# One chain of heads across the block borders, other yield distances in S5, and the short convolution of blocks 2 and 3 moved into the delta-rule groups

## The chip, the cores and the metric

The kernel runs on one core of a Trainium2 chip. The metric is the device time of one execution in microseconds (us). The kernel before took 2914.17 us (median of 3 runs, 2912.3 to 2915.87).

A core has several engines that each work through a queue of their own in order: TensorE (PE, matrix products; PEld is its weight load), VectorE (DVE), ScalarE (ACT), GpSimd (POOL) and SyncE (SP, which here issues the DMAs). An instruction waits at the head of its queue until what it needs is there, and all that stands behind it on the same engine waits with it.

## The reference

One layer of a hybrid encoder runs over 2048 prompt tokens and 32 decode tokens of a second request group, model width 1024, float32. All three mixers read the same normalised input through one projection; their outputs go together through `w_out`:

```python
hn = rmsnorm(h, norm_mix);  proj = hn @ w_in
qkv_pre, z, ba, u5, cc = split(proj)
ya = gdn_mixer(qkv_pre, z, ba, ...)   # short causal conv (4 taps) + silu on q, k, v; delta rule, 4 heads x 128
yb = s5_mixer(u5, ...)                # diagonal SSM, 16 groups, gelu, GLU
yc = conformer_conv(cc, ...)          # GLU, depthwise conv of 31 taps, LayerNorm, swish
h = h + concat([ya, yb, yc]) @ w_out
hf = rmsnorm(h, norm_ffn)
h = h + (silu(hf @ ffn_w1) * (hf @ ffn_w3)) @ ffn_w2
h = h + (p @ pe_w) * sigmoid(h @ pe_gate_w)
y = rmsnorm(h, norm_final)
```

The delta rule carries a 128 x 128 state per head along the tokens, and S5 a complex state, so both go through the blocks in order. The 32 decode tokens have states of their own.

## The kernel before

**Blocks and phases.** The 2080 tokens are cut into four blocks of 512 columns; the last also holds the 32 decode tokens and has 544, worked in two pieces of 272. Phase A (`PhaseA.block`) runs for blocks 0 to 3 and makes the projections: u5, the conformer's gate and value, twelve q/k/v tiles (`conv`, L592-620) and four z tiles. Phase F (`PhaseF.block`, L1107-1223) then runs for blocks 0 to 3: `w_out`, the 22 hidden tiles of the FFN, `w2`, the layer embedding and its gate. Every weight product is split into high and low parts and made in three passes (`dense`, L104, its matmuls at L120): a matmul of 128 x 512 is one of 528 in a phase A block and of 2016 in an F block, 272 columns wide twice over in block 3. These are the *dense* matmuls below.

**Heads.** Between the two phases stand the heads, which only need phase A's results and must be done before `w_out` of their block:
- `s5_init` (L207) builds the tables of S5 once; `s5_unit` (L415) runs S5 for two blocks at a time (unit 0: blocks 0 and 1; unit 1: blocks 2 and 3). It makes four rounds of ps_v, a scan on DVE that ends in X, and ps_y; after every second round a gelu that ends in gq; at the end ps_glu.
- `conformer_block` (L791), called conf(b) below: 31 taps on DVE for each of two channel halves (cacc, L812-813), PE transposes (ps_ct, L824), LayerNorm statistics on DVE, a scaling on POOL (L840), PE transposes back (ps_cf, L843), affine and swish on ACT and DVE (cxn), and the store to mixT (L852).
- `gdn_group` (L855): the delta rule for 256 tokens, two groups a block, gdn(b) below; in block 3 a further group for the 32 decode tokens. It normalises, makes kk and the matrix U, transposes v (ps_vt, L928), sends U through DRAM, solves row by row on DVE (ct, cx, L951-952), doubles the inverse on PE (ps_q, ps_z), then per 128 tokens ps_ks, ps_vn, ps_s, ps_o, a normalisation, a transpose (ps_ot, L1078), the gate (zy, L1079) and the store to mixT (L1080).

**How data goes between them.** Phase A writes the convolved and silu'd q/k/v to a DRAM tensor `sild`, the gated z to `zgd`, the conformer's input to `xcd`. All heads write to `mixT[b]` in DRAM. `PhaseF.block(b)` begins with eight loads hb<-mixT (L1124), each split into fah and fal, after which the same buffers are loaded with the residual (L1126); the first dense product of `w_out` needs all eight.

**Who sets the order.** The heads are Python generators. `G.start` puts one into a list of chains; `dense` calls `G.step` with its columns, and every 9216 columns (18 matmuls of 512) each chain in the list is advanced by one (L1251-1269). A chain that has just yielded n sleeps for n advances; so the yields say how far apart its parts are placed among the dense matmuls. A phase A block brings about 29 advances, an F block 112. `G.flush()` advances all chains until they are done. A scheduler then fixes each engine's queue at build time, from priorities (dense work and heads alike run in the lowest class, `later`, in the order they were issued), a model of times, and the memory pools. The heads' pools open and close with the generator (`cc_b`, `gd_b`, `s5_u`, one stack side), so a head that starts later can have to wait for the memory of an earlier one.

Before, the order at top level was this: block 0 of phase A; `s5_init` without yields, in a class ahead of `later`; then one chain conf(0), gdn(0) from block 1 and `s5_unit` 0 from block 2; a flush after block 3. F block b starts the chain conf(b+1), gdn(b+1), to which F block 0 adds S5 unit 1 at its end, and each F block ends with a flush. So nothing of a head was left over a border.

Of the kernel before, what the change touches and what calls it, by code (L numbers as in the profile page):

```python
# [206 lines left out]
def s5_init(G, A, tp, pspool):  # L207
# [84 lines left out]


# [25 lines left out]


# [41 lines left out]


# [51 lines left out]
def s5_unit(G, A, u, wp, pspool):  # L415
# [14 lines left out]
    for jq in range(4):  # L430
# [18 lines left out]
        yield 2  # L449
# [56 lines left out]
        yield 2  # L506
# [31 lines left out]
        yield 2  # L538
# [24 lines left out]
class PhaseA:  # L563


    def __init__(self, G, A, ctx):
# [55 lines left out]
    def block(self, b):  # L622
# [92 lines left out]
        with G.later():  # L715
            for g in gs:
                for _ in g:
                    pass
# [3 lines left out]
        for h in range(NH):  # L722
            self.conv(8 + h, 8 + h, b, hf, hl_, bc, n, last, t0)
        for h in range(NH):
            w = load_weight(G, A.w_in[12 + h], KD, "z", h)
            zz = wp.tile([P, n], F32, tag="gacc", name="zz")
            for c0, cn in chunks_of(n):
                cs = slice(c0, c0 + cn)
                p_ = dense(G, G.psD, "pd", w, hf, hl_, ks, c0, cn)
                V.tensor_tensor(zz[:, cs], p_[:, :cn], bc[:, cs], op=ALU.mult)  # L730
            th = wp.tile([P, n], F32, tag="gth", name="zth", bufs=1)
            nc.scalar.activation(th, zz, AF.Tanh, scale=0.5)
            V.scalar_tensor_tensor(zz, th, 1.0, zz, op0=ALU.add, op1=ALU.mult)
# [121 lines left out]
def gdn_group(G, A, sp, pspool, T, tw, nt, nw, S, b, c_out):  # L855
# [106 lines left out]
    yield 3  # L962
# [264 lines left out]
def trunk_kernel(ctx: ExitStack, tc: tile.TileContext, A):  # L1227
# [57 lines left out]
    G.sild = [dd.tile([P, 12, n], F32, tag=f"sild{b}", name=f"sild{b}") for b, n in enumerate(G.ns)]  # L1285
# [85 lines left out]
    with ExitStack() as cx:  # L1371
        pa = PhaseA(G, A, cx)
        pa.block(0)
        with R("s5i") as tp, G.heads():
            s5_init(G, A, tp, G.psM)

        with R("s5_0") as w5:
            G.start(run(conf_of(0), gdn_of(0)))
            for b in range(1, NB):
                if b == G.UB:  # L1380
                    G.start(s5_unit(G, A, 0, w5, G.psM))
                pa.block(b)
            if NB == G.UB:
                G.start(s5_unit(G, A, 0, w5, G.psM))
# [124 lines left out]
```

## Time and profile before

| | |
|---|---|
| median of 3 runs | 2914.17 us (2912.3 to 2915.87) |
| profiled execution, own time | 2906.6 us |
| its span | 2904.8 us |
| mean granted clock of TensorE | 0.976 |
| PE busy | 2775.6 us, 96% |
| DVE busy | 1769.2 us, 61% |
| ACT busy | 931.4 us, 32% |
| POOL busy | 625.4 us, 22% |
| PE idle, in the first 707 us (phase A) | 66 us |
| PE idle, 1160 to 1385 us (end of F block 0, start of F block 1) | 28 us |

The span is the time from the first to the last recorded instruction of one profiled execution. In a row of the profile, `out<-in` are the program's names without buffer numbers, `128x512` the partitions by elements of the output, and a time in square brackets the idle time of the engine ahead of that row with what ended it. "busy" of PE includes time in which it ran at a lower granted clock; the clock stands beside it in the table of stretches.

### The profile page before, as it was taken

The page shows a single profiled execution, that of the slowest core. Times are in us where ns is not written, and L with a number is a line of the kernel's source. Part 1 is how long each engine was busy: PE and PEld are TensorE (multiplying, and loading weights), DVE is VectorE, ACT ScalarE, POOL GpSimd, SP SyncE. Part 2 cuts the span into 40 slices and gives each one's busy share as a digit, 9 for nine tenths or more (in the row PEclk, how much of TensorE's full clock was granted, in tenths as well). Part 3 has the DMA queues.
Part 4 walks back from the last instruction along what each step waited for, and adds up shares of the span by engine and source line. Part 5 has one row for each costly group of instructions (what it writes and reads, how often), then busy time and mean ns, then how long its engine had stood idle before and what let it go on. Part 6 is the DMA issues. An engine that isn't in the chain of part 4 may idle for free.

```text
span 2904.8 us, 40874 instructions
## 1 busy us (share of the span) xinstructions
PE 2775.6 (96%) x15300; PEld 2373.5 (82%) x15300; DVE 1769.2 (61%) x3812; ACT 931.4 (32%) x1382; POOL 625.4 (22%) x482
## 2 busy tenths in 40 slices
PE   7789999899999999898999999999999999999997
PEld 5668777798878778676888887888888789999997
DVE  8989768896675856676663645954454543333343
ACT  4244433334322222233322323432222343222232
POOL 5733222133543434441010100110000010000000
PEclk9989999999999999899999999999999999999998
DMA  6577776657654546565565656765565574555553
GB/s 217 186 261 245 234 206 222 190 169 242 218 176 161 187 152 225 172 205 204 190 199 160 208 167 222 243 203 179 186 190 167 178 269 158 175 174 175 175 188 104
DMA packets 280566, 565.16 MB, mean 195 GB/s; under 512 B 68993, under 2 KB 128529, under 8 KB 280225
## 3 DMA queue, kind: packets, MB, share of 16 engines
q1 hardware_dynamic: 280368, 562.55, 60.1%
q8 instruction: 121, 1.98, 0.3%
q14 instruction: 77, 0.62, 0.1%
HBM read 457.67 MB, written 104.20 MB: 193 GB/s over the span
## 4 chain that ended last, share of the span: by engine, by line
PE 73%; DVE 14%; DMA 8%; issue 2%; SPq 2%; ACT 1%; POOL 0%; DVEq 0%; ACTq 0%; POOLq 0%
PE ps_d L120 65%; DVE gacc L614 1%; DVE cx L952 1%; DMA sild<-gacc 1%; DMA cu<-ud 1%; DVE ct L951 1%; PE ps_q L982 1%; DMA xk<-in_xT 1%; DMA mixT<-zy 1%; PE ps_z L995 1%; DVE cacc L813 1%; PE ps_kk L904 1%; DMA zy<-zgd 1%; DVE X L498 1%; PE ps_ks L1025 1%
## 5 line engine op out<-in xcount | busy, mean ns | idle before, releaser
L94 ACT ACTIVATE wh_w<-wr_w 128x1024 fp32r<-128x1024 f32 (+1 forms) x272 | 281.3, 1034 | 841.3 <-PE ps_d L120 596.5
L120 PE MATMUL ps_d<-fah,wh_w 128*128 128x512 f32 (+1 forms) x1760 | 382.0, 355 | 7.8 <-DVE hb L1142 3.4
L120 PE MATMUL ps_d<-fal,wh_w 128*128 128x512 f32 (+1 forms) x1760 | 379.2, 354 | 0.0
L120 PE MATMUL ps_d<-fah,wl_w 128*128 128x512 f32 (+1 forms) x1760 | 375.5, 352 | 0.0
L120 PEld LDWEIGHTS ps_d<-fah,wh_w 128*128 128x128 f32 x1760 | 290.7, 189 | 52.4 <-issue 4.9
L120 PEld LDWEIGHTS ps_d<-fal,wh_w 128*128 128x128 f32 x1760 | 291.4, 189 | 42.7
L120 PEld LDWEIGHTS ps_d<-fah,wl_w 128*128 128x128 f32 x1760 | 290.8, 188 | 42.8
L1187 DVE TENSOR_TENSOR hb<-hb,ps_d 128x512 f32<-128x512 f32 (+1 forms) x240 | 140.1, 585 | 181.7 <-PE ps_d L120 180.7
L120 PE MATMUL ps_d<-acth,wh_w 128*128 128x512 f32 (+1 forms) x880 | 208.3, 355 | 8.0 <-DVE hb L1187 4.5
L96 POOL TENSOR_TENSOR wl_w<-wr_w,wh_w 128x1024 fp32r<-128x1024 f32 (+1 forms) x68 | 160.7, 2365 | 237.3 <-ACT wh_w L94 229.5
L120 PE MATMUL ps_d<-acth,wl_w 128*128 128x512 f32 (+1 forms) x880 | 209.4, 354 | 0.0
L120 PE MATMUL ps_d<-actl,wh_w 128*128 128x512 f32 (+1 forms) x880 | 209.1, 355 | 0.0
L813 DVE SCALAR_TENSOR_TENSOR cacc<-xc,cc_w,cacc 128x512 f32<-128x512 f32 (+1 forms) x240 | 178.8, 779 | 0.0
L120 PEld LDWEIGHTS ps_d<-acth,wh_w 128*128 128x128 f32 x880 | 148.8, 189 | 34.3 <-DVE hb L1187 6.9
L120 PEld LDWEIGHTS ps_d<-actl,wh_w 128*128 128x128 f32 x880 | 150.1, 190 | 22.4
L120 PEld LDWEIGHTS ps_d<-acth,wl_w 128*128 128x128 f32 x880 | 149.8, 189 | 22.3
L1170 DVE SCALAR_TENSOR_TENSOR fth<-ps_d,bc 128x512 f32<-128x512 f32 (+1 forms) x110 | 64.8, 589 | 135.4 <-PE ps_d L120 134.8
L1165 DVE TENSOR_TENSOR fa<-ps_d,bc 128x512 f32<-128x512 f32 (+1 forms) x110 | 64.7, 589 | 128.8 <-PE ps_d L120 115.5
L1168 DVE SCALAR_TENSOR_TENSOR fa<-fth,fa 128x512 f32<-128x512 f32 (+1 forms) x110 | 92.3, 839 | 73.4 <-ACT fth L1167 73.2
L614 DVE SCALAR_TENSOR_TENSOR gacc<-raw,cw,gacc 128x512 f32<-128x512 f32 (+1 forms) x144 | 118.9, 828 | 27.4 <-ACT gacc L612 24.8
L1173 DVE TENSOR_TENSOR actl<-fa,acth 128x512 fp32r<-128x512 f32 (+1 forms) x110 | 85.5, 778 | 48.6 <-ACT acth L1172 48.4
L120 PE MATMUL ps_d<-hh,wl_qkv 128*128 128x512 f32 (+1 forms) x480 | 108.2, 362 | 5.9 <-POOL wl_qkv L96 5.9
(468 smaller groups left out, 4817.1 us busy)
## 6 DMA issues: line engine op xcount, KB each, us to landing
wr_w<-in_w SPq DMA_DIRECT2D x256, 512.0 KB, 4.0
wl_w<-lo_w SPq DMA_DIRECT2D x192, 512.0 KB, 3.5
lo_w<-wl_w SPq DMA_DIRECT2D x64, 512.0 KB, 3.0
wr_qkv<-in_w_in SPq DMA_DIRECT2D x48, 512.0 KB, 4.0
wl_qkv<-lo_qkv SPq DMA_DIRECT2D x36, 512.0 KB, 4.3
wr_out<-in_w_out SPq DMA_DIRECT2D x32, 512.0 KB, 4.9
wr_gate<-in_pe_gate SPq DMA_DIRECT2D x32, 512.0 KB, 4.6
sild<-gacc SPq DMA_DIRECT2D x48, 256.0 KB, 4.1
```

What stands on the lines that cost most here:

```text
L94: nc.scalar.activation(wh, wr, AF.Copy)
L96: nc.gpsimd.tensor_tensor(wl, wr, wh.bitcast(F32), op=ALU.subtract)
L120: nc.tensor.matmul(ps[:, :cn], a[:, i, :], x(k)[:, c0:c0 + cn], start=start and p_ == 0 and i == 0, stop=stop and p_ == 2 and i == K - 1)
L498: V.tensor_tensor(X[h][half[i], :, 1:], a[half[h], :, :NC], b_[half[h], :, :NC], op=op)
L614: V.scalar_tensor_tensor(acc, raw[:, t:t + W], cw[:, m, t:t + 1], acc, op0=ALU.mult, op1=ALU.add)
L813: V.scalar_tensor_tensor(acc[:, j], xc[:, j, t:t + W], cn_.w[:, j, t:t + 1], acc[:, j], op0=ALU.mult, op1=ALU.add)
L904: nc.tensor.matmul(kk4[:, h - h0], kq[:, 2 * h, cw], kq[:, 2 * h:2 * h + 2, cw], start=True, stop=True)
L1165: V.tensor_tensor(a, p1[:, :cn], bc[:, cs], op=ALU.mult)
L1168: V.scalar_tensor_tensor(a, th, 1.0, a, op0=ALU.add, op1=ALU.mult)
L1170: V.scalar_tensor_tensor(th, p3[:, :cn], 0.5, bc[:, cs], op0=ALU.mult, op1=ALU.mult)
L1173: V.tensor_tensor(fb[:, cs], a, fa[:, cs].bitcast(F32), op=ALU.subtract)
L1187: V.tensor_tensor(hb[m][:, c0:c0 + cn], hb[m][:, c0:c0 + cn], p_[:, :cn], op=ALU.add)
```

## The change

Six edits (the lines of after.py stand some 9 to 53 further down; L822 there is L813 of before):
1. `s5_init` becomes a generator with ten yields or so. It heads a chain `first_heads`: `s5_init`, gdn(0), conf(0), in that order, started before block 1; the conformer is now last. `first_s5` starts at block 2 and waits until the memory of S5 is open. Their flush stands after block 3 as before.
2. One chain `later_heads` runs over all F blocks: conf(1), gdn(1), conf(2), S5 unit 1, gdn(2), conf(3), gdn(3). Ahead of F block b it is only advanced until gdn(b) is done, so a head may go on over a border.
3. The yields in `s5_unit` go from 2, 2, 2 to 3, 4, and 1 or 5; the yield behind the row solve in `gdn_group` from 3 to 5.
4. For blocks 2 and 3 (`G.raw`), `conv` stores its raw tile and returns. `gdn_group` loads three raw tiles, makes the four taps (ACT and three DVE instructions per tile and head), tanh and the silu product, with four further yields of 2 a group.
5. The rest of the gates' computation (`for _ in g`) comes after the twelve conv tiles, not before them.
6. The conv's weights become a constant of the whole kernel.

By its yields, `first_heads` needs 93 advances where blocks 1 to 3 bring some 90, and `later_heads` needs 342 up to the end of gdn(3) where F blocks 0 to 2 bring 336.

```diff
--- before.py
+++ after.py
@@ s5_unit @@
-        yield 2
+        yield 3
...
-        yield 2
+        yield 4
...
-        yield 2
+        yield 1 if jh == 0 else 5
@@ PhaseA.conv @@
+        if b in G.raw:
+            nc.sync.dma_start(G.sild[b][:, jj], raw)
+            return
@@ gdn_group @@
+    if b in G.raw:
+        c0 = c_out + (3 if c_out >= BLK else 0)
+        raws = [sp.tile([P, 4, nn + 3], F32, tag=tg, name="raw" + tg, bufs=1) for tg in ("AQ", "X", "XT")]
+        for i in range(3):
+            nc.sync.dma_start(raws[i], G.sild[b][:, 4 * i:4 * i + 4, c0:c0 + nn + 3])
+        yield 2
+        for i, dst in enumerate((kq[:, 0:4], kq[:, 4:8], vf)):
+            for x in range(4):
+                m = 8 + x if i == 2 else (2 * i + x // 2) + (4 if x % 2 == 0 else 0)
+                a = dst[:, x]
+                nc.scalar.activation(a, raws[i][:, x, 0:nn], AF.Copy, scale=G.cw[:, m, 0:1])
+                for t in range(1, 4):
+                    V.scalar_tensor_tensor(a, raws[i][:, x, t:t + nn], G.cw[:, m, t:t + 1], a, op0=ALU.mult, op1=ALU.add)
+            th = sp.tile([P, 4, nn], F32, tag="U", name="cth", bufs=1)
+            nc.scalar.activation(th, dst, AF.Tanh)
+            V.scalar_tensor_tensor(dst, th, 1.0, dst, op0=ALU.add, op1=ALU.mult)
+            yield 2
...
-    yield 3
+    yield 5
@@ top level, phase A @@
-        with R("s5i") as tp, G.heads():
-            s5_init(G, A, tp, G.psM)
-        with R("s5_0") as w5:
-            G.start(run(conf_of(0), gdn_of(0)))
...
+        def first_heads():
+            with R("s5i") as tp:
+                yield from s5_init(G, A, tp, G.psM)
+            with R("s5_0") as w5:
+                box["w5"] = w5
+                yield from gdn_of(0)
+                yield from conf_of(0)
+                while "done" not in box:
+                    yield 1
@@ top level, phase F @@
-            G.start(run(conf_of(nb), gdn_of(nb), *(s5_of(u) ...)))
-        pf.block(b)
-        G.flush()
+    def later_heads():
+        for b in range(1, NB):
+            yield from conf_of(b)
+            if b % G.UB == 0:
+                yield from s5_of(b // G.UB)
+            yield from gdn_of(b)
+            ready[0] = b
+    G.start(later_heads())
+    for b in range(NB):
+        G.flush(lambda: ready[0] >= b)
+        pf.block(b)
```

The order of the queues at the border between phase A and phase F, on DVE. Before, behind the last z tile (zz; L730 its eviction, L733 its gate) come the splits of F block 0 (fal, L1105), the end of conf(1) (cxn_7722) and the first eviction of `w_out` (hb, L1142):

```order
L730 TENSOR_TENSOR zz_6987<-ps_d_6988,bc_5114 128x272
L730 TENSOR_TENSOR zz_6987<-ps_d_7014,bc_5114 128x272
L1105 TENSOR_TENSOR fal_7077<-hb_7085,fah_7069 128x512
L1105 TENSOR_TENSOR fal_7079<-hb_7095,fah_7071 128x512
L1105 TENSOR_TENSOR fal_7081<-hb_7105,fah_7073 128x512
L1105 TENSOR_TENSOR fal_7083<-hb_7115,fah_7075 128x512
L1105 TENSOR_TENSOR fal_7084<-hb_7120,fah_7076 128x512
L733 SCALAR_TENSOR_TENSOR zz_6987<-zth_7040,zz_6987 128x544
L851 SCALAR_TENSOR_TENSOR cxn_7722<-cth_7724,cxn_7722 128x512
L1142 TENSOR_TENSOR hb_7085<-hb_7085,ps_d_7134 128x512
```

After, at the same place (L739 and L742 are L730 and L733 of before, L822 the taps; cacc_6213 is conf(0), cacc_6936 conf(1); L836 to L844 are conf(0)'s statistics, L860 its swish):

```order
L739 TENSOR_TENSOR zz_6709<-ps_d_6710,bc_4744 128x272
L822 SCALAR_TENSOR_TENSOR cacc_6213<-xc_6210,cc_w_149,cacc_6213 128x512
L739 TENSOR_TENSOR zz_6709<-ps_d_6742,bc_4744 128x272
L822 SCALAR_TENSOR_TENSOR cacc_6936<-xc_6934,cc_w_149,cacc_6936 128x512 x2
L822 SCALAR_TENSOR_TENSOR cacc_6213<-xc_6210,cc_w_149,cacc_6213 128x512 x2
L822 SCALAR_TENSOR_TENSOR cacc_6936<-xc_6934,cc_w_149,cacc_6936 128x512
L742 SCALAR_TENSOR_TENSOR zz_6709<-zth_6784,zz_6709 128x544
L822 SCALAR_TENSOR_TENSOR cacc_6213<-xc_6210,cc_w_149,cacc_6213 128x512 x46
L836 BN_STATS cst_6749<-ctk_6743 128x6
L837 BN_AGGR cmv_6744<-cst_6749 128x2
```

Behind the last eviction of phase A now stand 51 taps, 48 of them conf(0)'s, and then all of conf(0)'s statistics; before, conf(0) was long done there. The store of conf(0) to mixT[0] and behind it the eight loads hb<-mixT[0] stand on SP after that.

The same at the border between F blocks 2 and 3, on PE. Before, ps_vn of the decode group stood among the `w2` products (acth, actl) of F block 2, 288 dense matmuls ahead of the block's end:

```order
L120 MATMUL ps_d<-acth,wh_w_19996 128x512 x4
L120 MATMUL ps_d<-acth,wl_w_19997 128x512 x4
L120 MATMUL ps_d<-actl,wh_w_19996 128x512 x4
L1038 MATMUL ps_vn<-rk,X 32x128 x4
L120 MATMUL ps_d<-acth,wh_w_20030 128x512 x2
L120 MATMUL ps_d<-acth,wl_w_20031 128x512 x2
```

After (L1065, L1079, L1105 are L1038, L1052, L1078 of before), between the last gate product of F block 2 and the first of `w_out` of block 3:

```order
L120 MATMUL ps_d<-fah,wh_gate 128x512 x8
L120 MATMUL ps_d<-fah,wl_gate 128x512 x8
L120 MATMUL ps_d<-fal,wh_gate 128x512 x8
L1065 MATMUL ps_vn<-rk,X 32x128 x4
L149 MATMUL ps_ss<-ones,ssum_20034 128x1 x4
L1072 MATMUL ps_s<-vn,rk 128x128 x4
L1079 MATMUL ps_o<-Sd_19706,kq 32x128
L1080 MATMUL ps_o<-vn,AQ 32x128
...
L132 MATMUL ps_bc<-ident,rso 128x128 x4
L1105 MATMUL ps_ot<-ident,o 128x32 x4
L120 MATMUL ps_d<-fah,wh_out 128x272 x22
```

The last part of the decode group, ps_vn to ps_ot, moved from among dense products to behind all of them; ps_vt of the same group stands 124 dense matmuls ahead of the border. In S5 unit 1 the dense matmuls between ps_v and the ps_y that needs X are 51, 48, 54, 51 before (at the end of F block 0) and 75, 47, 55, 52 after (at the start of F block 1); between the last ps_y and the second group of ps_glu 112 before and 92 after. Between the last ps_ot of gdn(2) and the border of F blocks 1 and 2 stand 58 dense matmuls after.

More of the change, by code (lines that the diff above doesn't have):

```diff
@@ L318, in s5_init @@
     cmul(nc, [x[:, :, :16] for x in big], Bre, Bim, bre0, bim0, bc(kre), bc(kim))
+    yield 1
     C.Hre = cp.tile([P, 8, 9, 16], F32, tag="Hre", name="Hre")
@@ L327, in s5_init @@
         cmul(nc, tmp, C.Hre[:, :, l], C.nHim[:, :, l], cre0, cim0, bc(Lre[:, l]), bc(Lim[:, l]))
+        if l % 3 == 2:
+            yield 1
     V.tensor_scalar(C.nHim, C.nHim, -1.0, None, op0=ALU.mult)
@@ L361, in s5_init @@
         nc.sync.dma_start(C.Toep[l * 16:(l + 1) * 16, :, (7 - l) * 16:P].rearrange("p g (l c) -> p g l c", c=16), kg[:, :, 0:l + 1])
+    yield 1
     NC = G.UB * BLK // L5
@@ L381, in s5_init @@
         m *= 2
+        yield 1
     a = big[0][:, :, :NC]
@@ L714, in block @@
                 nc.sync.dma_start(G.xcd[b + 1][:, j, 0:30], xc[:, BLK - 30:BLK])
[L715 to L718, printed above, removed]
         for h in range(NH):
@@ L723, in block @@
             self.conv(8 + h, 8 + h, b, hf, hl_, bc, n, last, t0)
+        with G.later():
+            for g in gs:
+                for _ in g:
+                    pass
         for h in range(NH):
@@ L864, in gdn_group @@
     kq = sp.tile([P, 8, nn], F32, tag="kq", name="kq", bufs=1)
-    nc.sync.dma_start(kq, G.sild[b][:, 0:8, c_out:c_out + nn])
     vf = sp.tile([P, NH, nn], F32, tag="vf", name="vf", bufs=1)
-    nc.sync.dma_start(vf, G.sild[b][:, 8:12, c_out:c_out + nn])
+    if b in G.raw:
[14 more added lines that the diff above has]
+            V.scalar_tensor_tensor(dst, th, 1.0, dst, op0=ALU.add, op1=ALU.mult)
+            yield 2
+    else:
+        nc.sync.dma_start(kq, G.sild[b][:, 0:8, c_out:c_out + nn])
+        nc.sync.dma_start(vf, G.sild[b][:, 8:12, c_out:c_out + nn])
     yield 2
@@ L1265, in step, with flush @@
             G.chains = [c for c in G.chains if advance(c)]
-    def flush():
-        while G.chains:
+    def flush(done=lambda: False):
+        while G.chains and not done():
             G.chains = [c for c in G.chains if advance(c)]
@@ L1284, in trunk_kernel @@
     G.mixT = [dd.tile([P, KD, n], F32, tag=f"mixT{b}", name=f"mixT{b}") for b, n in enumerate(G.ns)]
-    G.sild = [dd.tile([P, 12, n], F32, tag=f"sild{b}", name=f"sild{b}") for b, n in enumerate(G.ns)]
+    G.raw = set(range(2, NB))
+    wid = lambda b: G.ns[b] + (3 + 3 * (b == NB - 1) if b in G.raw else 0)
+    G.sild = [dd.tile([P, 12, wid(b)], F32, tag=f"sild{b}", name=f"sild{b}") for b in range(NB)]
     G.zgd = [dd.tile([P, NH, n], F32, tag=f"zgd{b}", name=f"zgd{b}") for b, n in enumerate(G.ns)]
@@ L1315, in trunk_kernel @@
         G.strict = const("strict", [P, P], A.c_strict)
+        G.cw = const("cw", [P, 12, 4], A.conv_w, half=True)
         G.mhalf = cp.tile([P, 1], F32, tag="mhalf", name="mhalf")
@@ L1373, in trunk_kernel, with first_s5 @@
         pa.block(0)
-        with R("s5i") as tp, G.heads():
-            s5_init(G, A, tp, G.psM)
-        with R("s5_0") as w5:
-            G.start(run(conf_of(0), gdn_of(0)))
[L1379 to L1384, printed above, removed]
-            G.flush()
-    pf = PhaseF(G, A, ctx)
+        box = {}
+        def first_s5():
+            while "w5" not in box:
+                yield 1
+            yield from s5_unit(G, A, 0, box["w5"], G.psM)
+            box["done"] = True
+        def first_heads():
[6 more added lines that the diff above has]
+                while "done" not in box:
+                    yield 1
+        G.start(first_heads())
+        for b in range(1, NB):
+            if b == G.UB:
+                G.start(first_s5())
+            pa.block(b)
+        if NB == G.UB:
+            G.start(first_s5())
+        G.flush()
+    pf = PhaseF(G, A, ctx)
+    ready = [0]
+    def later_heads():
+        for b in range(1, NB):
+            yield from conf_of(b)
[4 more added lines that the diff above has]
+    G.start(later_heads())
     for b in range(NB):
-        nb = b + 1
-        if nb < NB:
-            G.start(run(conf_of(nb), gdn_of(nb), *(s5_of(u) for u in range(1, G.NU) if max(u * G.UB - 2, 0) == b)))
+        G.flush(lambda: ready[0] >= b)
         pf.block(b)
-        G.flush()
 def _layout(np, d):
```

3 lines of the change are left out of this document (1 added, 2 removed).

## Prediction

> **What bounds the kernel now.** I began with the page's slices, to see where PE is not full or not at full clock. All times are in us of the one profiled execution (span 2904.8).
>
> ```profile
> PE   7789999899999999898999999999999999999997
> ...
> DVE  8989768896675856676663645954454543333343
> ...
> PEclk9989999999999999899999999999999999999998
> ```
>
> PE is the bound nearly everywhere; what it loses lies in the first quarter and near the 17th slice. DVE is fullest there too. The table of stretches, cut at the borders of the phases, gives it in numbers (columns: stretch, length, then busy of PE, PEld, DVE, ACT, POOL, then granted clock):
>
> ```profile
> 0.00:191.00 191.00, 155.89 (x649) 119.23 (x650) 167.73 (x405) 68.14 (x101) 114.06 (x110) 0.92 0.67 220
> 191.00:707.00 516.00, 485.13 (x2848) 414.40 (x2846) 416.62 (x995) 193.62 (x313) 139.32 (x163) 0.97 0.68 214
> 707.00:1160.00 453.00, 441.50 (x2127) 362.67 (x2126) 297.45 (x495) 131.14 (x184) 196.42 (x89) 0.99 0.58 191
> 1160.00:1385.00 225.00, 197.23 (x871) 159.04 (x870) 154.33 (x273) 73.46 (x108) 74.20 (x45) 0.90 0.59 190
> 1385.00:2300.00 915.00, 913.16 (x4451) 752.49 (x4449) 505.65 (x1186) 281.25 (x404) 74.07 (x57) 1.00 0.61 192
> 2300.00:2440.00 140.00, 135.83 (x824) 120.07 (x823) 61.67 (x105) 56.05 (x81) 15.84 (x12) 0.99 0.67 223
> ```
>
> Phase A (to 707) leaves PE idle for 35.1 + 30.9 = 66 and loses 0.08 x 156 + 0.03 x 485 = 27 to the clock: 93 that could be had. The end of F block 0, with S5 unit 1 in it (1160 to 1385), loses 27.8 idle and 0.10 x 197 = 20 of clock: 48. From 1385 on PE is full, borders included. The waits of PE name the causes (total, times, longest):
>
> ```profile
> PE ps_y L518 <- DVE X L498: 13.7, 3, 5.5
> PE ps_d L120 <- DVE zz L730: 13.4, 4, 4.9
> ...
> PE ps_glu L547 <- DVE gq L537: 8.7, 2, 6.4
> ...
> PE ps_q L982 <- DVE g_p L771: 4.2, 1, 4.2
> ```
>
> The first and the third are S5's own chain, the other two phase A's DVE. A wait costs more than itself:
>
> ```profile
> 84.52 2.00 PE L120 MATMUL ps_d<-hh,wh_qkv 128*128 128x512 f32 x8
> 92.47 3.78 PE L120 MATMUL ps_d<-hh,wl_qkv 128*128 128x512 f32 x8 [5.95 <-POOL wl_qkv L96]
> 96.05 2.63 PE L120 MATMUL ps_d<-hl,wh_qkv 128*128 128x512 f32 x8
> ```
>
> Eight matmuls of 512 columns start 1.84 apart at full clock (0.23 each); behind a pause of 5.95 two such rows take 3.58 and 2.47 to the next start, so a long pause adds about 2.4. The Trainium skill, "TensorE: Matmul & The Clock Gate", section "What's actually happening", states that after an idle window of about 3.4 us TensorE runs at half rate until it has been busy about as long, which would be an estimate of 1.7 a pause; the same page, "HAM oscillation", speaks against gaps above 3.4 us, and so against what this change leaves at its borders. By 1.7 the sum below would be 1.4 lower.
>
> **Part 1, the border between phases A and F.** Before there is no pause:
>
> ```profile
> 706.56 1.03 PE L843 MATMUL ps_cf<-ident,ctk 128*128 128x128 f32 x8
> ...
> 707.35 3.72 PE L120 MATMUL ps_d<-fah,wh_out 128*128 128x512 f32 x15
> ```
>
> In the new order 51 taps, 48 of them conf(0)'s, stand on DVE behind the eviction of the last z product, which PE has to finish first. PE has nothing else queued ahead of `w_out` than the transposes of conf(0) and conf(1), and `w_out` needs all eight hb loads, which stand on SP behind conf(0)'s stores. So nothing covers this chain. Its durations:
>
> ```profile
> 706.76 0.44 DVE L730 TENSOR_TENSOR zz<-ps_d,bc 128x272 f32<-128x272 f32 x1 [1.56 <-PE ps_d L120]
> 715.26 0.71 DVE L733 SCALAR_TENSOR_TENSOR zz<-zth,zz 128x544 f32<-128x544 f32 x1
> ```
> ```profile
> 191.65 3.40 DVE L813 SCALAR_TENSOR_TENSOR cacc<-xc,cc_w,cacc 128x512 f32<-128x512 f32 x5
> ```
> ```profile
> L813 DVE SCALAR_TENSOR_TENSOR cacc<-xc,cc_w,cacc 128x512 f32<-128x512 f32 x180 | 130.4, 757 | 0.0
> ```
> ```profile
> 683.14 0.60 PE L824 MATMUL ps_ct<-ident,cacc 128*128 128x128 f32 x4
> ...
> 691.25 2.19 POOL L840 TENSOR_SCALAR ctk<-ctk,rso,cnm 128x256 f32<-128x256 f32 x4 [1.12 <-DVE cnm L835]
> ...
> 711.05 0.76 ACT L846 ACTIVATE cxn<-ps_cf,cc_bb,cc_g 128x512 f32<-128x512 f32 x1
> ...
> 711.84 0.63 ACT L850 ACTIVATE cth<-cxn 128x512 f32<-128x512 f32 x1
> ...
> 715.89 0.68 DVE L851 SCALAR_TENSOR_TENSOR cxn<-cth,cxn 128x512 f32<-128x512 f32 x1
> ```
>
> A tap takes 0.68 in a row of five and 0.757 in the mean of 180; I take 0.72, so 0.44 + 51 x 0.72 + 0.71 = 37.9. From ps_ct to the end of the POOL scaling it is 691.25 + 2.19 - 683.14 = 10.3. Then ps_cf 1.03, 0.76, 0.63, 0.68, and the second half some 0.8 behind: 3.9. Then the transfers, from issue to landing (the last column), with SP's time to issue the eight loads:
>
> ```profile
> hb<-mixT SPq DMA_DIRECT2D x24, 256.0 KB, 6.7
> ...
> hb<-mixT SPq DMA_DIRECT2D x8, 272.0 KB, 4.6
> mixT<-cxn SPq DMA_DIRECT2D x6, 256.0 KB, 2.9
> ...
> mixT<-zy SPq DMA_DIRECT2D x1, 64.0 KB, 2.9
> ```
> ```profile
> 664.83 0.81 SPq L1124 DMA_DIRECT2D hb<-mixT  x2
> ...
> 666.16 3.39 SPq L1124 DMA_DIRECT2D hb<-mixT  x6
> ```
>
> The store takes 0.3 + 2.9. The eighth load is issued 0.81 + 3.39 = 4.2 after the first and lands 6.7 later; the seven matmuls that can run ahead of it take 1.8 off, and its split into fah adds about half a us: 9.6. Together 37.9 + 10.3 + 3.9 + 3.2 + 9.6 = 64.9, from which about 4.4 goes for PE's transposes, which are work either way: **+60** (45 if the taps begin earlier than the order says and the loads spread less, 72 if the taps take 0.757 and the second cxn waits).
>
> The Trainium skill, "DMA: Bandwidth & Descriptors", section "Anatomy of one DMA — SWDGE (gpsimd) path", fits about 2.0 us and the bytes over 436e3 a us, an estimate of 2.6 for 256 KB; by that this border would be 4 us shorter, the next 3, and the sum 41 in place of 48. The rows (2.9, 6.7, 4.6; issued from SP) decide.
>
> **Part 2, the border between F blocks 2 and 3.** The decode group of gdn(3):
>
> ```profile
> 2249.97 0.60 PE L928 MATMUL ps_vt<-ident,vf 128*32 128x128 f32 x4
> ...
> 2293.34 1.05 PE L1038 MATMUL ps_vn<-rk,X 32*32 32x128 f32 x8
> ...
> 2317.76 0.43 PE L1078 MATMUL ps_ot<-ident,o 32*128 32x32 f32 x4
> ```
> ```profile
> 2318.61 0.37 SPq L1080 DMA_DIRECT2D mixT<-zy  x1
> ```
>
> From ps_vt to ps_vn it takes 43.4: two trips through DRAM and the row solve. Now 124 dense matmuls stand there, 28.5, with some 1.7 of small ones: PE waits about 13. From ps_vn to the store it took 25.3 with dense products in between; with PE free I estimate 13, half of it, ends 8 and 25. Store 3.2; eight loads 4.2 + 4.6 - 1.0 and fah 0.6: 8.4. Sum 37.6, less about 4 of PE work: **+34** (22 to 45). Before, 288 dense matmuls (66 us) hid this tail.
>
> Both borders leave PE cold, 2 x 2.4: **+5** (2 to 8).
>
> **Part 3, less DVE work in phase A.** The conv of blocks 2 and 3 leaves it:
>
> ```profile
> L614 DVE SCALAR_TENSOR_TENSOR gacc<-raw,cw,gacc 128x512 f32<-128x512 f32 x108 | 91.0, 844 | 18.4 <-ACT gacc L612 16.2 <-POOL tails L608 0.8
> ```
>
> By that row a third, block 2, is 30 of DVE, block 3 about as much, and the silu product goes too. But PE only waited on DVE there for a part: zz 13.4 and g_p 4.2, 17.6 in all. With about half of the 27 of clock that such pauses cost: **-30**. Ends: -10, if other waits follow (the first 191, with DVE at 88%, keep `s5_init`, which still lies ahead of gdn(0) in DVE's order), and -50. All of the 93 is a rival.
>
> **Part 4, S5 unit 1 from the end of F block 0 to the start of block 1.** What it lost, 48, goes there; but the matmuls that stand between ps_v and ps_y are 75, 47, 55 and 52 where they were 51, 48, 54 and 51, and the second ps_glu is nearer (92, was 112). Three of four gaps are as short, so I expect some 13 of stalls and 10 of ramps again: **-25** (0 to -45). gdn(1), with its longer sleep, keeps its place among the first dense matmuls of F block 0.
>
> **Part 5, the conv inside the groups.** In 1385 to 2300 DVE is busy 506 of 915, and PE does not wait; the groups get longer, which the two borders already show. At the border of blocks 1 and 2 the 58 matmuls (13.3) behind the last ps_ot stand against zy 0.7, store 3.5, loads and split about 9.6: 13.8. **+4** (0 to 12). The gates' move and the constant cost nothing: they are small and DVE has room behind the conv tiles.
>
> **Sum.** 60 + 34 + 5 - 30 - 25 + 4 = **+48**: a span of 2953, and on the median, which lies 7.6 above the profiled execution's own 2906.6, 2914.2 + 48 = **2962**.
>
> **The rivals.**
> - *Phase A gives back what the borders take* (faster). If the pauses of phase A vanish whole, with their ramps, part 3 is -93 and the sum 60 + 34 + 5 - 93 - 25 + 4 = -15: 2899. It decides from -78 on. For it: DVE is the fullest engine there, and 76% busy would become less. Against it: only 17.6 of the 66 idle us are waits on DVE that the moved work feeds, and the first 191 hardly change. 10%.
> - *S5 gains nothing*: its gaps are as short as before, part 4 is 0, the sum +73: 2987. For it the distances; against it that F block 1's start has less else on DVE. 12%.
> - *The border of blocks 1 and 2 stalls as well*, as the loads are behind a late store by one DVE queue: another 12, 2974. For it 13.8 against 13.3; against it that the order places it before the last products. 10%.
> - *The relief is near 60 and the borders are at their low ends*: no difference, 2914. 5%.
>
> **The numbers.** My own case has 63%. Its terms' half-widths, 13, 12, 3, 20, 22 and 6, make 35 if added as squares, so 2927 to 2997; the rivals of S5 and of the third border lie within or near it. I give 2924 to 3000, which leaves out the faster rival and the even case. A difference of 0.2%, 6 us, is what a measurement of this kernel can tell. Faster 0.10, same 0.05, slower 0.85.
>
> **What would show it.** In the new profile: a pause of PE of some 60 just ahead of the first `w_out` of F block 0, with 46 taps in one row on DVE in it; one of about 30 in two pieces ahead of `w_out` of block 3, around ps_vn and ps_ot; waits ps_y on X still there, shortly after the border of F blocks 0 and 1; a clock below 0.9 at each. Phase A's dense part would end some 30 earlier than 706. I am wrong if `w_out` of block 0 starts within 20 of the last z product, or if phase A ends 80 earlier.

## The result

The changed kernel takes 2963.06 us (median of 4 runs, 2960.63 to 2966.64) against 2913.78 us before (4 runs, 2912.3 to 2915.87): a ratio of 1.017, 95% interval 1.0152 to 1.0187. It is slower, 1 us above the forecast 2962 and inside the range of 2924 to 3000. The span of its profiled execution is 2960.1 us, 55.3 more than before; forecast were 48 more. That the median comes within 1 us of the forecast is partly chance: I had put it 9.4 above the span, as in the kernel before; here it is 3.0 above.

The slices of the page, as for the kernel before:

```profile
PE   7799999992999989799999999999999979999997
...
DVE  8966737478684755976464664966374653333343
...
PEclk9899999995999999899999999999999979999998
```

Two holes are new, in the 10th slice (PE at 2, clock at 5) and in the 33rd. The table of stretches of the changed kernel, cut at its own borders (same columns as before: stretch, length, busy of PE, PEld, DVE, ACT, POOL, granted clock):

```profile
0.00:191.00 191.00, 154.62 (x650) 117.88 (x651) 171.10 (x403) 69.63 (x104) 106.46 (x109) 0.92 0.65 217
191.00:676.50 485.50, 470.46 (x2819) 404.88 (x2816) 303.86 (x815) 154.96 (x247) 98.70 (x153) 0.99 0.71 223
676.50:736.50 60.00, 9.63 (x34) 4.86 (x33) 47.74 (x88) 7.95 (x15) 9.45 (x11) 0.53 0.18 59
...
1190.00:1305.00 115.00, 99.30 (x401) 77.57 (x400) 99.69 (x127) 40.87 (x62) 52.17 (x27) 0.93 0.47 159
1305.00:1500.00 195.00, 193.43 (x951) 157.55 (x950) 116.98 (x270) 70.48 (x100) 32.24 (x28) 1.00 0.76 240
...
2385.00:2421.50 36.50, 15.24 (x63) 9.83 (x61) 14.82 (x35) 4.52 (x7) 6.61 (x5) 0.61 0.44 149
```

Phase A's dense part ends at 676.6 us, 30 earlier than before; then PE stands nearly still for 60 us and the clock falls to 0.53. S5 unit 1, now in 1305 to 1500, runs with PE full. The end of F block 0 (1190 to 1305) has a loss of its own. Ahead of F block 3 stands the second hole. The waits of PE (total, times, longest):

```profile
PE ps_ct L833 <- DVE cacc L822: 39.0, 1, 39.0
PE ps_d L120 <- DVE raw L613: 17.2, 5, 6.1
PE ps_d L120 <- DVE hb L1214: 14.2, 9, 3.0
PE ps_ot L1105 <- DVE o L1097: 10.1, 1, 10.1
...
PE ps_vn L1065 <- DMA X<-xd: 5.4, 1, 5.4
...
PE ps_d L120 <- DVE zz L739: 4.2, 2, 2.6
...
PE ps_y L525 <- DVE X L505: 1.0, 1, 1.0
```

The first is conf(0)'s taps, the fourth and the fifth the decode group. ps_y on X fell from 13.7 to 1.0, zz from 13.4 to 4.2; larger are raw (q/k/v evictions of block 0; 2.4 before) and hb (5.5 before; 10.7 of the 14.2 are w2 evictions at the end of F block 0).

The border of phases A and F, from the timeline (start, length, engine, line):

```profile
675.79 0.82 PE L120 MATMUL ps_d<-hl,wh_z 128*128 128x272 f32 x4
...
677.78 3.10 POOL L96 TENSOR_TENSOR wl_out<-wr_out,wh_out 128x1024 fp32r<-128x1024 f32 x1 [7.59 <-ACT wh_out L94]
...
678.95 2.47 DVE L822 SCALAR_TENSOR_TENSOR cacc<-xc,cc_w,cacc 128x512 f32<-128x512 f32 x1
...
681.35 0.43 DVE L739 TENSOR_TENSOR zz<-ps_d,bc 128x272 f32<-128x272 f32 x1
...
685.65 30.55 DVE L822 SCALAR_TENSOR_TENSOR cacc<-xc,cc_w,cacc 128x512 f32<-128x512 f32 x46
...
715.59 1.35 PE L833 MATMUL ps_ct<-ident,cacc 128*128 128x128 f32 x4 [38.98 <-DVE cacc L822]
...
722.95 2.30 PE L852 MATMUL ps_cf<-ident,ctk 128*128 128x128 f32 x8 [4.63 <-POOL ctk L849]
...
732.18 3.49 SPq L1151 DMA_DIRECT2D hb<-mixT  x7
...
735.40 0.63 ACT L1130 ACTIVATE fah<-hb 128x512 fp32r<-128x512 f32 x1 [4.37 <-DMA hb<-mixT]
...
736.46 0.78 PE L120 MATMUL ps_d<-fah,wh_out 128*128 128x512 f32 x1
```

The last z product is evicted late (681.35), behind a tap that takes 2.47 beside a subtraction on POOL. The 46 taps stand in one row, and everything behind them is a chain in which PE mostly waits (9.6 us busy of 60). The border of F blocks 2 and 3:

```profile
2386.36 2.00 PE L120 MATMUL ps_d<-fal,wh_gate 128*128 128x512 f32 x8
...
2393.77 1.91 PE L1065 MATMUL ps_vn<-rk,X 32*32 32x128 f32 x8 [5.41 <-DMA X<-xd]
...
2405.89 6.39 DVE L1249 SCALAR_TENSOR_TENSOR hb<-hb,g,bc 128x512 f32<-128x512 f32 x5
...
2415.12 0.63 PE L1105 MATMUL ps_ot<-ident,o 32*128 32x32 f32 x4 [10.10 <-DVE o L1097]
...
2418.00 3.65 SPq L1151 DMA_DIRECT2D hb<-mixT  x8
...
2421.53 1.82 PE L120 MATMUL ps_d<-fah,wh_out 128*128 128x272 f32 x6 [5.78 <-ACT fah L1130]
```

33.1 us from the end of the last gate product (2388.4) to `w_out`: 5.4 for X, 21.4 from ps_vn to ps_ot, 6.4 from there to `w_out`. Within the 21.4 the five hb products of F block 2's own output stand on DVE ahead of the decode group's normalisation.

### The profile page after: what moved, and what is told of

Read it like the earlier page. It is cut to its first block, busy times and chain, and to the rows that moved or that the text cites. A ratio compares the mean times of both kernels' runs of the same rounds, so it can differ in the third digit from the quotient of the medians.

```text
span 2960.1 us, 40926 instructions
## 1 busy us (share of the span) xinstructions
PE 2771.8 (94%) x15300; PEld 2365.2 (80%) x15300; DVE 1775.6 (60%) x3911; ACT 939.2 (32%) x1409; POOL 585.6 (20%) x482
## 4 chain that ended last, share of the span: by engine, by line
PE 67%; DVE 11%; DMA 4%; ACT 1%; issue 1%; SPq 1%; POOL 0%; DVEq 0%; ACTq 0%; POOLq 0%
PE ps_d L120 59%; DVE cacc L822 4%; DVE cx L979 1%; PE ps_q L1009 1%; DVE ct L978 1%; DVE hb L1214 1%; PE ps_kk L931 1%; PE ps_z L1022 1%; DMA mixT<-zy 1%; DMA hb<-mixT 1%; DMA cu<-ud 1%; PE ps_o L1079 0%; PE ps_o L1080 0%; PE ps_s L1072 0%; PE ps_vn L1065 0%
## 5 line engine op out<-in xcount | busy, mean ns | idle before, releaser
L822 DVE SCALAR_TENSOR_TENSOR cacc<-xc,cc_w,cacc 128x512 f32<-128x512 f32 (+1 forms) x240 | 194.4, 858 | 0.0
L120 PEld LDWEIGHTS ps_d<-acth,wh_w 128*128 128x128 f32 x880 | 148.3, 189 | 46.8 <-issue 13.5
L120 PE MATMUL ps_d<-hh,wh_qkv 128*128 128x512 f32 (+1 forms) x480 | 109.3, 368 | 16.0 <-DVE raw L613 15.8
L1199 ACT ACTIVATE acth<-fa 128x512 fp32r<-128x512 f32 (+1 forms) x110 | 60.3, 548 | 154.0 <-DVE fa L1198 153.9
```

Source lines behind the costliest of these rows:

```text
L120: nc.tensor.matmul(ps[:, :cn], a[:, i, :], x(k)[:, c0:c0 + cn], start=start and p_ == 0 and i == 0, stop=stop and p_ == 2 and i == K - 1)
L822: V.scalar_tensor_tensor(acc[:, j], xc[:, j, t:t + W], cn_.w[:, j, t:t + 1], acc[:, j], op0=ALU.mult, op1=ALU.add)
L1199: nc.scalar.activation(fa[:, cs], a, AF.Copy)
```

## The experiments

Twelve kernels, each run beside the kernel before. The times at which PE reaches the same places of the program, read from its timeline, in us of each profiled execution:

| kernel | block 2 of A begins | last z product ends | first w_out of F block 0 | F blocks 0 and 1 | F block 2 with its border | ratio to before |
|---|---|---|---|---|---|---|
| before | 337.8 | 706.7 | 707.4 | 1128.5 | 531.9 | |
| changed | 326.9 | 676.6 | 736.5 | 1116.9 | 568.1 | 1.017 |
| e1 | 325.2 | 675.1 | 702.1 | 1112.7 | 568.2 | 1.0035 (1.0024 to 1.0047) |
| e3 | 341.8 | 696.3 | 696.5 | 1112.1 | 567.9 | 1.0033 (1.0019 to 1.0046) |
| e4 | 330.3 | 704.8 | 766.0 | 1113.2 | 541.0 | 1.0162 (1.0143 to 1.0181) |
| e5 | 323.3 | 677.8 | 717.8 | 1106.3 | 533.2 | one run: 2897.87 us, before 2909.96 |
| e6 | 338.5 | 709.8 | 710.4 | 1106.7 | 535.0 | 0.9932 (0.9914 to 0.9951) |
| e7 | 322.9 | 672.3 | 699.4 | 1111.6 | 566.5 | one run: 2919.05 us, before 2909.96 |
| e8 | 339.8 | 703.5 | 703.4 | 1106.0 | 539.2 | 0.9925 (0.9902 to 0.9949) |
| e9 | 339.9 | 701.8 | 701.9 | 1107.2 | 534.3 | 0.9909 (0.9894 to 0.9925) |
| e10 | 332.1 | 706.4 | 747.1 | 1133.5 | 530.0 | 1.0117 (1.0094 to 1.014) |
| e11 | 338.7 | 720.7 | 720.9 | 1116.8 | 530.0 | 1.0001 (0.9986 to 1.0017) |
| e12 | 338.9 | 707.2 | 707.8 | 1088.9 | 529.9 | one run: 2866.48 us, before 2910.98 |
| e13 | 340.4 | 710.6 | 711.2 | 1071.9 | 541.1 | 0.9858 (0.984 to 0.9876) |

"F blocks 0 and 1" runs from the first `w_out` of block 0 to that of block 2, the next column from there to that of block 3. Phase A is the same program in before, e6, e12 and e13 (707.4, 710.4, 707.8, 711.2), so a difference there under 4 us says nothing. The last F block takes 536 to 540 in all. e10's profiled execution is the longest of its four (2950.5, the median is 2942.62), so its row may lie some us too high.

**e1, conf(0) ahead of gdn(0).**

```diff
-                yield from gdn_of(0)
                 yield from conf_of(0)
+                yield from gdn_of(0)
```

> The changed kernel with one thing altered: conf(0) goes ahead of gdn(0) in the first chain, so that the 46 taps no longer stand behind the last z product; what stands there now is the end of gdn(0), from ps_s of its last window on. Theory (the pause of 60 us at the border of phases A and F is conf(0)'s place in the chain, and the 30 us that phase A ends earlier come from the conv that left it): phase A's dense part still ends near 677 us, the pause shrinks to some 30 us (the normalisation of gdn(0), its store and the eight loads), total near 2933 us. Rival (phase A only ended earlier because the taps were put off): its dense part ends near 700 us, and the total stays near 2960 us.

The dense part ends at 675.1 and `w_out` begins 27.0 later, not 59.9: the theory's places held, and the total, 2920.3, is lower than it said. The pause has changed hands: conf(1)'s transposes wait for POOL, then PE waits for gdn(0)'s last store.

```profile
674.97 0.60 PE L833 MATMUL ps_ct<-ident,cacc 128*128 128x128 f32 x4
...
686.01 1.23 PE L852 MATMUL ps_cf<-ident,ctk 128*128 128x128 f32 x4 [7.33 <-POOL ctk L849]
...
702.07 1.65 PE L120 MATMUL ps_d<-fah,wh_out 128*128 128x512 f32 x3 [11.65 <-ACT fah L1130]
```

**e3, raw q/k/v alone** (before with edits 4 to 6).

```diff
+        if b in G.raw:
+            nc.sync.dma_start(G.sild[b][:, jj], raw)
+            return
```

> The kernel before with edits 4 to 6 alone: raw q/k/v for blocks 2 and 3, the conv in the delta-rule groups; the chains and yields are the old ones. Theory (the relief of phase A is the conv, and the pause ahead of block 3 is the conv too, as it makes gdn(3) longer, and not the chain over the borders): phase A's dense part ends 20 to 30 us earlier than 706.7 us with no pause at its end, S5 unit 1 stalls as before, PE pauses some 30 us around ps_vn ahead of block 3; total 2905 to 2920 us. Rival (the pause ahead of block 3 comes from the one chain, and the relief from putting conf(0) off): phase A ends near 700 us, no pause ahead of block 3, total near 2910 us by other parts; the two are told apart by the two places in the trace.

Half of the theory fell. The conv takes only 10.4 us off the dense part (14 off block 3, nothing off block 2, and blocks 0 and 1 take 4 more), not 20 to 30. The pause ahead of block 3 is there without any of the new chains, 27.0 from the last gate product to `w_out`, so it comes from edits 4 to 6:

```profile
2347.41 2.00 PE L120 MATMUL ps_d<-fal,wh_gate 128*128 128x512 f32 x8
2349.34 1.06 PE L1058 MATMUL ps_vn<-rk,X 32*32 32x128 f32 x8
...
2376.40 1.79 PE L120 MATMUL ps_d<-fah,wh_out 128*128 128x272 f32 x6 [13.27 <-ACT fah L1123]
```

S5 unit 1, at its old place with its old yields, lost less than before: F blocks 0 and 1 took 16 us less. Its gaps between ps_v and ps_y were 58 to 60 dense matmuls in this kernel, where they were 48 to 54, and only one of its X is slow (2.37 us), where four were before (2.00 to 2.57).

**e4, raw q/k/v for block 2 only**, on the changed kernel.

```diff
-    G.raw = set(range(2, NB))
+    G.raw = {2}
```

> The changed kernel with raw q/k/v for block 2 only; block 3's conv stays in phase A. Theory (the conv made gdn(3) too long): the pause of 33 us ahead of block 3 goes; phase A gets the 30 us or so of block 3's conv back on DVE, of which 10 to 15 us show; total near 2940 us. Rival (the yields of the one chain, 342 advances against 336, make the pause): it stays at 20 us or more, and the total is 2960 us or more.

The pause ahead of block 3 is gone (F block 2 takes 541.0, 27 less), so the yields of edit 3 did not make it. But the total, 2957, is near the rival's 2960: block 3's conv came back whole to DVE ahead of the taps, and `w_out` of block 0 begins 30 us later still.

```profile
PE ps_ct L833 <- DVE cacc L822: 40.3, 1, 40.3
...
PE ps_d L120 <- DVE zz L739: 19.2, 1, 19.2
```

**e5, e1 without raw q/k/v at all**, and **e7, e1 with the old yields of S5.**

```diff
 # e5
-    G.raw = set(range(2, NB))
+    G.raw = set()
 # e7, in s5_unit
-        yield 3
+        yield 2
...
-        yield 4
+        yield 2
...
-        yield 1 if jh == 0 else 5
+        yield 2
```

> The kernel of run e1 (conf(0) ahead of gdn(0)) without raw q/k/v: the conv of all blocks stays in phase A. In phase A blocks 0 and 1 took 326 us before and 313 us in e1, blocks 2 and 3 369 us before and 350 us in e1. Theory (the relief has two parts: s5_init in pieces instead of in one run on DVE gives the first 10 to 13 us, the conv the rest): block 2 begins near 326 us as in e1, blocks 2 and 3 take 365 us or more again. Rival (all of it is the conv): block 2 begins near 337 us as before.

> The kernel of run e1 with the old yields of S5 (2, 2, 2). Theory (the longer yields only move S5 unit 0 from block 2 into block 3): blocks 2 and 3 together take 350 us within 4 us, and phase A's dense part ends near 675 us. Rival (the longer yields take S5's stalls away in phase A): it ends 8 us or more later, with waits of ps_y on X or of ps_glu on gq.

In e5 block 2 begins early (323.3), as the theory said, but blocks 2 and 3 take 354.5, not 365, and the dense part ends at 677.8 with the whole conv in phase A. So that end says little: the dense products end early because heads were put behind them. `w_out` begins 40 later, at 717.8. The fair measure is the start of `w_out`, and by it the conv is worth 15.7 here (717.8 against 702.1). e7 went by its theory: 349.4 for blocks 2 and 3 (349.9 in e1), end at 672.3.

**e6, the one chain over the F blocks alone** (before with edit 2).

```diff
-            G.start(run(conf_of(nb), gdn_of(nb), *(s5_of(u) ...)))
-        pf.block(b)
-        G.flush()
+    G.start(later_heads())
+    for b in range(NB):
+        G.flush(lambda: ready[0] >= b)
+        pf.block(b)
```

> The kernel before with edit 2 alone: the one chain over the F blocks, with the old yields of S5 (2, 2, 2) and of the row solve, and the conv in phase A. Theory (S5's stalls went because of the place, where DVE has less to do, not because of the longer yields): the waits of ps_y on X fall from 13.7 us to under 3 us as in the changed kernel, conf(2)'s taps cost some 15 us at the end of F block 0, net 8 to 14 us faster than before: 2900 to 2906 us. Rival (the longer yields did it): the waits on X stay above 10 us, and the time is 2914 us or more.

The rival is out: with the yields 2, 2, 2, ps_y waits for no X any more, and F blocks 0 and 1 take 22 us less. The total, 2890.6, is lower than the theory's 2900 to 2906. conf(2)'s cost is there as expected, at the end of F block 0:

```profile
PE ps_d L120 <- DVE hb L1187: 13.1, 8, 3.0
...
PE ps_d L120 <- DVE fth L1170: 4.3, 1, 4.3
```

**e8 and e9, e6 with raw q/k/v for one block.** e8 adds edits 4 to 6 with `G.raw = {2}`; e9 with `G.raw = {3}`, and there the decode tokens are convolved in phase A:

```diff
+    G.raw = {3}
...
         if b in G.raw:
             nc.sync.dma_start(G.sild[b][:, jj], raw)
+            if last:
+                acc = wp.tile([P, W], F32, tag="gacc", name="gacc")[:, :TS]
...
+                nc.sync.dma_start(G.sildd[:, jj], acc)
             return
```

> The kernel of run e6 (one chain over the F blocks) with raw q/k/v for block 2 only and the old order in phase A. Run e3 took no time out of block 2 of phase A (192.5 us, before 192.7) and 14 us out of block 3 (162.0, before 176.2). Theory (the conv is only on the path in block 3): no gain over e6, 2888 to 2893 us. Rival (DVE's load in block 2 is what makes phase A late): 2876 to 2884 us.

> The kernel of run e6 with raw q/k/v for block 3 only, and there for the prompt's groups only: the decode tokens' conv stays in phase A, on 32 columns a tile. By the order the last ps_ot of the decode group stands 54 dense matmuls (12.4 us) ahead of the border of F blocks 2 and 3. Theory (the conv counts in block 3 of phase A, and only a late end of gdn(3) costs at the border): phase A ends 10 to 14 us earlier than in e6 and there is no pause above 4 us ahead of block 3: 2876 to 2884 us, the fastest of all. Rival (what phase A gives, gdn(3) takes back): a pause of 10 us or more at that border, 2888 us or more.

e8: 2886.89; its interval and e6's overlap, so no gain is shown. e9: 2883.63, no pause ahead of block 3, phase A 8 us shorter where the theory said 10 to 14; it too is not clear of e6.

```profile
2341.57 2.00 PE L120 MATMUL ps_d<-fal,wh_gate 128*128 128x512 f32 x8
2343.41 1.14 PE L120 MATMUL ps_d<-fah,wh_out 128*128 128x272 f32 x7
```

**e10, the first chain alone** (before with edit 1), and **e11, S5's yields alone.**

```diff
 # e10
+        def first_heads():
+            with R("s5i") as tp:
+                yield from s5_init(G, A, tp, G.psM)
...
+        G.start(first_heads())
 # e11, in s5_unit
-        yield 2
+        yield 3
...
-        yield 2
+        yield 4
...
-        yield 2
+        yield 1 if jh == 0 else 5
```

> The kernel before with edit 1 alone: s5_init in pieces at the head of the chain, gdn(0) ahead of conf(0); the conv stays in phase A, the F blocks keep their old chains and yields. In its order 21 taps of conf(0) stand behind the last z product. Theory (this edit makes the pause at the border of phases A and F, and also gives blocks 0 and 1 their 11 to 14 us): block 2 begins near 326 us (before 337.8), a pause of 35 to 45 us stands ahead of the first w_out, which starts 25 to 40 us later than before, S5 unit 1 stalls as before, nothing stands ahead of block 3: total 2932 to 2948 us. Rival (the pause needs the conv's move, since the raw tiles let the dense part end before the taps): w_out of block 0 starts within 10 us of 707 us, total within 10 us of before.

> The kernel before with the longer yields of S5 alone (3, 4, 1 or 5). Theory (they hardly move anything in the F blocks: by the order ps_v of S5 unit 1 stands 24 to 32 dense matmuls later than before, at the same distances): F blocks 0 and 1 take 1128 us as before within 6 us, total 2904 to 2914 us. Rival (room for S5 is what counts, at the old place too): ps_y's waits on X fall under 4 us and the total to 2890 to 2898 us.

e10: 2942.62; a pause of 40.7, `w_out` 39.7 later than before, S5 unit 1 stalled as ever. Only blocks 0 and 1 gained less than the theory's 11 to 14, some 6. e11: no change in the total, as the theory said, but not for its reason. F blocks 0 and 1 lose 12 us less, and phase A takes 13.5 more. The distances did not stay the same either: in the trace 58 to 60 dense matmuls stand between ps_v and ps_y, as in e3, and again one X is slow (2.37).

```profile
PE ps_ct L831 <- DVE cacc L820: 19.7, 1, 19.7
PE ps_y L525 <- DVE X L505: 15.6, 3, 5.7
```
```profile
PE ps_d L120 <- DVE raw L607: 9.1, 3, 5.6
...
PE ps_y L518 <- DVE X L498: 5.7, 3, 4.7
```

The first fence is e10, the second e11.

**e12, low halves of F block 0 on ACT; e13, e6 with these low halves on DVE.** The open question was why the same gaps stall at the end of F block 0 and not in F block 1. In the kernel before, POOL and DVE side by side there:

```profile
1161.22 5.03 POOL L96 TENSOR_TENSOR wl_w<-wr_w,wh_w 128x1024 fp32r<-128x1024 f32 x2
...
1161.48 2.57 DVE L498 TENSOR_TENSOR X<-tm,tm 64x256 f32<-64x256 f32 x1
...
1166.30 0.42 DVE L498 TENSOR_TENSOR X<-tm,tm 64x256 f32<-64x256 f32 x1
```

The same X takes 2.57 beside POOL's subtraction and 0.42 after it. Only F block 0 makes low halves; the later blocks load them.

```diff
 # e12, in load_weight, for the weights of the F blocks
-            nc.gpsimd.tensor_tensor(wl, wr, wh.bitcast(F32), op=ALU.subtract)
...
+                nc.scalar.activation(wl, wr, AF.Copy)
 # e13, besides edit 2
-            nc.gpsimd.tensor_tensor(wl, wr, wh.bitcast(F32), op=ALU.subtract)
+            e = nc.gpsimd if name in ("qkv", "z", "u5", "ccg", "cca") else nc.vector
+            e.tensor_tensor(wl, wr, wh.bitcast(F32), op=ALU.subtract)
```

> The kernel before with one thing altered: in F block 0 the low halves of the weights are not made by POOL's subtraction but by a copy on ACT (so the low halves' subtraction is left out there and the output is another); S5 unit 1 stays at the end of F block 0 with its old yields, its gaps between ps_v and ps_y are 48, 38 to 44, 60 and 30 to 34 dense matmuls by the order, no longer than before. Theory (S5's DVE work is slow in F block 0 because POOL works at the same time: an X took up to 2.57 us there, 0.42 in the median): no X above 0.8 us, the waits of ps_y on X fall under 5 us in spite of the shorter gaps, F block 0 takes 560 to 572 us where it took 584. Rival (the heads ahead of it on DVE hold it up, POOL or not): waits of 10 us or more remain, F block 0 takes 578 us or more.

> The kernel of run e6 (one chain over the F blocks, the conv in phase A) with the low halves of F block 0's weights made by DVE instead of POOL; nothing is left out. On POOL such a subtraction takes 2.4 us and DVE's instructions stand still beside it. Theory (it costs DVE about 1.2 us in place of a stretch of 2.4 us in which it is held up): F blocks 0 and 1 together, 1107 us in e6 and 1089 us in run e12, take 1090 to 1102 us; total 2876 to 2887 us. Rival (the subtractions then stand in DVE's queue ahead of the evictions that PE waits for): 1107 us or more, total 2890 us or more.

e12 leaves the low halves' subtraction out in F block 0. S5 unit 1 stands at its old place, with gaps of 48, 38, 60 and 30 dense matmuls (51, 48, 54 and 51 before); no X takes more than 0.8, and ps_y waits 1.3 on X:

```profile
PE ps_y L521 <- DVE X L501: 1.3, 2, 1.1
```

F block 0 takes 549 us in place of 584, less than the theory's 560 to 572. DVE's busy time in it falls from 389 to 284 with nothing taken from DVE.

```profile
707.00:1270.00 563.00, 555.29 (x2706) 455.54 (x2705) 284.43 (x684) 261.94 (x340) 59.75 (x45) 0.99 0.60 200
```
```profile
707.00:1291.80 584.80, 557.45 (x2659) 458.42 (x2658) 388.57 (x676) 170.26 (x242) 256.49 (x125) 0.96 0.57 188
```

The first row is e12 (to a little beyond the end of F block 0, which was at 1257), the second the kernel before. e13 computes all that the kernel before computes and is the fastest: 2865.23 us, ratio 0.9858 (0.984 to 0.9876). A subtraction costs DVE 1.2 us:

```profile
L97 DVE TENSOR_TENSOR wl_w<-wr_w,wh_w 128x1024 fp32r<-128x1024 f32 (+1 forms) x68 | 81.8, 1203 | 14.0 <-ACT wh_w L94 12.4 <-DMA wr_w<-in_w 0.5 <-DMA hb<-mixT 0.5
```

F blocks 0 and 1 take 1072 in e13, below the 1090 to 1102 that the theory gave and 35 less than in e6.

## Why the prediction was right, and where it was not

On the same cut as the table, the forecast was +32 at the start of `w_out` (60 of the border, 2.4 of ramp, less 30), -21 for F blocks 0 and 1 (-25 and +4), +36 for F block 2 and its border, 0 behind it. Measured are +29.1, -11.6, +36.2 and +1.5, together 55.2.

1. **Border of phases A and F, +60: right in mechanism and place; the size agrees by errors that cancel.** From the last z product to `w_out` it takes 59.9 (0.7 before). For the same stretch the forecast had 64.9, before 4.4 went off for transposes that PE makes in it. The wait for the taps was 39.0, forecast 37.9: a tap took 0.66 in the long row, not 0.72, but the eviction of the last z product ended 5.2 after that product, not 0.44. From ps_ct to the issue of the loads it took 16.6, forecast 17.4 (10.3, 3.9 and 3.2). The loads took 4.3 from issue to the first product, not 9.6: PE began as soon as the first of the eight was there, and 21 products, not seven, ran before the eighth was needed, with a wait of 0.28. The ramp behind the pause was 1.6 (the 21 products took 6.4, where 0.23 each make 4.8), not 2.4. e1 shows that the order of the two heads makes the larger part of the pause: the start of `w_out` moves 34 earlier.
2. **Phase A's relief, -30: the number came, but it is no measure of the conv.** The forecast put the 30 down to DVE having less to do. The dense part does end 30.1 earlier. But e5 ends it at 677.8 with the whole conv in place, and e3, with the conv gone, only at 696.3; there the waits that the forecast took off whole, zz 13.4 and g_p 4.2, are still 9.9 and 4.3. By the start of `w_out` the conv is worth 11 (before to e3), 15.7 (e5 to e1), and 29.5 for block 3's alone in the order of the changed kernel (e4 to the changed kernel). So its worth depends on what else stands there, and the +29 has no single split. Measured are +40 for edit 1 alone (e10) and -11 for the other edits on top of it; among these the yields of S5, which by themselves cost phase A 13.5 (e11), are mixed with the conv. Part of the 30 is work that went behind the last z product, and so is part of the 60 of step 1; how much was not measured. Had conf(0) stood elsewhere, my sum would have missed this.
3. **Border of F blocks 2 and 3, +34: right** (33.1; the forecast for the same stretch was 37.6, before 4 went off for PE's work), and e3 and e4 show its cause: moving block 3's conv lengthens gdn(3) until its end falls behind the block; neither the one chain nor the yields of edit 3 are needed for it. Edit 4 lengthens gdn(3) in two ways, by the conv's own work on DVE and by the yields it brings: eight advances in each of three groups are 432 dense matmuls, where 288 stood behind ps_vn before. No run takes the two apart; e9, which leaves both out for the decode group, has no pause. The parts were off both ways: 5.4 in place of 13 ahead of ps_vn, 21.4 in place of 13 for the tail, 6.4 in place of 11.6 for store and loads. The tail is long because F block 2's output products stand ahead of it on DVE, which I had not counted.
4. **S5 unit 1, -25: half of it reached the changed kernel, and my reason failed.** I expected some 13 of stalls to stay, because the gaps were as short; 1.0 stayed on X. e6 shows that the new place is enough, with the old yields, and e12 why the old place was bad: POOL's low halves hold DVE up in F block 0. Longer gaps at the old place help in part (e3, e11: X 5.5 and 5.7). What I did not see is the other side of the move: conf(2) now does its taps at the old place, and PE waits 10.7 on hb and 4.3 on fth there (1.7 and nothing before). It is the same hold-up: in e6 21 of conf(2)'s taps overlap a subtraction on POOL and take 1.57 in the mean, where the other 159 taps of that width take 0.76; in e13, with conf(2) at the same place and no such subtraction on POOL, 4.7 on hb and nothing on fth are left there. F blocks 0 and 1 gain 22 in e6 and 12 in the changed kernel. The rival "S5 gains nothing" is out.
5. **Border of F blocks 1 and 2, inside +4: right in size.** A pause of 3.1. That the gates' move and the constant cost nothing did not hold in the old order of phase A: in e3, e8 and e9, where they stand without edit 1, block 1 begins 4 to 5 us later than before (200.4 to 200.6, before 195.7).
6. **The faster rival** (phase A gives all back) would have needed 78 us and more; by the start of `w_out` the edits together cost 29. DVE was busy for 584 of the first 707 us, 83% and not 76%; nothing in the sum hangs on it.

Two things stay open. Why the dense part ends so early in e1, e5 and e7 (672 to 678), whether the conv stands there or not, was not taken apart further. Nor was it found which of the other edits costs the 6 to 10 us by which F blocks 0 and 1 are longer in the changed kernel and e1 than in e6.

## What to carry to other kernels

When the order of queued work changes, count what stands behind the last instruction that the next phase has to wait for, on each engine; a yield count, or an earlier end of the phase before, says nothing by itself. Cost a phase by the start of the next one and not by the end of its own dense part: work that is put off looks like a gain until the border. Where a chain stalls at one place and not at another with the same distance, compare the same instruction's duration at both places, and see what other engine is busy beside it.

## What was not expected of the hardware

- **POOL holds DVE up.** An X takes 0.42 us by itself and 2.57 beside subtractions on POOL of some 2.5 each; the same subtraction takes 1.2 us on DVE itself. The Trainium skill, "SBUF — State Buffer", section "SBUF: two separate sides", states that DVE and GpSimd share a pair of ports that is locked for a whole instruction, and that a DVE instruction with two SBUF inputs and a GpSimd instruction that reads SBUF block each other by it; the rows, e12 and e13 agree. DVE's "busy" in a profile contains this standing still, an estimate of some 105 us of the 389 in F block 0 by e12.
- **The first of eight loads comes early, the others do not.** At the two borders the first split began 3.2 and 2.8 us after the issue of the first load. But the seventh load at the border of phases A and F landed 6.0 after its issue, and the sixth and seventh ahead of F block 3 landed 4.6 and 4.9 after theirs, about as the medians before (6.7 and 4.6). The 2.6 that the prediction worked out as an estimate from the fit of the Trainium skill, "DMA: Bandwidth & Descriptors", section "Anatomy of one DMA — SWDGE (gpsimd) path", is near the first load alone; for the others, all issued from SP, the measured times decide.
- **A tap takes 0.66 us** in an undisturbed row (30.55 for 46), where the mean before was 0.757.
